# Transposing FFN activations on VectorE in squares of 32 instead of on TensorE, in a two-layer decoder trunk

## The chip, the core and the metric

The kernel runs on one core of a Trainium2 chip. The core has a matrix engine (TensorE, "PE" in the profile, with its weight loads as "PEld"), VectorE ("DVE"), ScalarE ("ACT"), GpSimd ("POOL"), and SyncE ("SP"), which here only issues DMA transfers. The metric is the device time of one execution in microseconds (us), lower is better; a run's number is the median of several executions.

## What is computed

The reference is a trunk of two layers on 256 tokens of width 2048, all in float32. What matters here is the dense SwiGLU feed-forward network (FFN) that ends each layer, with an inner width of 5632, and the projections around it:

```
for i in range(DEPTH):                       # DEPTH = 2
    mixer = even_mixer if i % 2 == 0 else odd_mixer
    h = h + mixer(rms_norm(h, ...), ...)
    h = h + swiglu(rms_norm(h, ffn_norm[i]), ffn_w_gate[i], ffn_w_up[i], ffn_w_down[i])
return rms_norm(h, final_norm)

def swiglu(hn, w_gate, w_up, w_down):
    return (jax.nn.silu(hn @ w_gate) * (hn @ w_up)) @ w_down
```

The even mixer is attention beside a gated delta rule, the odd mixer a gated MLP over positions; the change touches neither.

## The kernel before

The 256 tokens are two token tiles of 128 partitions (`NT` = 2). Widths are cut into chunks of 512 (`CW`): the model's 2048 are 4 chunks (`NCH`), the FFN's 5632 are 11 (`NFF`). A matmul contracts over partitions, so what is multiplied by a weight must lie with its features on the partitions: it must be transposed. The kernel calls such a transposed chunk a unit: for each token tile a pair of tiles of 128 features by 4 blocks by 128 tokens, a high part rounded to the reduced type `fp32r` and a low part with the rest (`split`: ScalarE casts `hi`, VectorE subtracts to get `lo`).

`dense` multiplies units by weights. For each unit it loads a piece `raw` of 512 rows of weights (1 MB, by SP, 3 buffers), and for each of its 4 blocks of 128 rows splits it: ScalarE casts `whi`, VectorE subtracts to get `wlo` (6 buffers each). TensorE then does three matmuls for each token tile (high by high, high by low, low by high), so six for each block, each 128 by 128 against 512 columns.

`ffn` runs over the 11 chunks: `dense` with the gate weights, SiLU on ScalarE into `sg`, `dense` with the up weights, a multiplication on VectorE (SCALAR_TENSOR_TENSOR) into `sg`, and `fill_unit`, which makes the unit of the chunk. `fill_unit` transposes with TensorE, four blocks of 128 by 128 for each token tile against the identity matrix `ident` into the PSUM buffers `side`, and then splits. `project` is the down projection (and the mixers' output projections): for each of 4 chunks of the output one `dense` over all units, an addition into the residual `h`, and, unless it is the last layer, `fill_unit` of the new residual with the next norm's gain, which makes the next stage's units.

No engine's order is written by hand. Every operation is recorded with a planned cost and a priority (`prio`; lower goes first among operations that are ready), and `plan` simulates engines, DMA and buffers, and fixes each engine's order and each tile's buffer. Weight splits have priority 0, `fill_unit` and what surrounds it 1, matmuls of `dense` 9. A tile gets a buffer only when one is free, and when all tiles recorded before it can still be held: an operation that is recorded late but waits for nothing, such as the load of the final norm's gain (`load_final`, `swdge` on POOL), may start as soon as that allows. There are 58 buffers `unit` and 4 `wide`, each of 4 KB on a partition at the most.

All operations are issued from one line (178, the recorder's call), so the profile's groups differ by tile names, not by lines.

Of the kernel before, what the change touches and what calls it, by code (L numbers as in the profile page):

```python
# [10 lines left out]
F32R = mybir.dt.float32r  # L11
BF16 = mybir.dt.bfloat16
AF = mybir.ActivationFunctionType
ALU = mybir.AluOpType
AX = mybir.AxisListType

P = 128
D = 2048
SEQ = 256
NT = SEQ // P  # L20
KB = 4
CW = 512
NCH = D // CW
# [29 lines left out]
NFF = DFF // CW  # L53
# [8 lines left out]
C_TRI, C_TB, C_SU, C_H0, C_DMASK, C_ONE, C_AM, C_LVL, C_UP, C_SAME, C_DIAG = 0, 1, 2, 3, 4, 5, 6, 8, 10, 11, 12  # L62
NCONST = 16
LAG = 10
SB = 16


# [208 lines left out]
class Engine:  # L276
# [5 lines left out]
    def __getattr__(self, name):  # L282
        f = getattr(self.engine, name)

        def record(*args, **kw):
            aps = [a for a in (*args, *kw.values()) if isinstance(a, bass.AP)]
            size = lambda a: a.free_size()
            n, k, table, nbytes = size(aps[0]), self.key, None, 0
            scalars = sum(size(a) == 1 for a in aps[1:])
            if name == "dma_start":  # L290
                cost, nbytes = (1040.0 if k == "pool" else 60.0), 4 * P * n
            elif k == "pe":
                cost = 3.0 + (107.0 if name == "transpose" else
                              (1.0 if aps[1].dtype == F32R and n >= 256 else 4.0) * n / 2.4)
            elif k == "act":
                given = sum(not isinstance(kw.get(x, 0.0), float) for x in ("scale", "bias"))
                cost = (51.0 if aps[1].space == bass.MemoryType.PSUM else 93.0) + 0.833 * n + 93.0 * given
                if name == "activation":
                    table = self.schedule.TABLES.get(args[2])
                    cost += 93.0 * ("accum_out" in kw)  # L300
            elif k == "dve":
                n = size(aps[1]) if name in ("tensor_reduce", "bn_stats") else n
                cost = 69.0 + (0.521 if name == "tensor_scalar" else 1.042) * n + 60.0 * scalars
            else:
                cost = 165.0 * n + 320.0 if ALU.pow in args else 1.9 * n + 200.0
            self.schedule.record(k, f, args, kw, cost, table, nbytes)

        return record
# [6 lines left out]
class Trunk:  # L315
# [135 lines left out]
    def fill_unit(self, srcs, gain=None):  # L451
# [10 lines left out]
            self.split(ps, unit[t])  # L462
        return unit


    def dense(self, w, units, off, width=CW, pcs=None, lag=0, first=False):

        nc = self.nc  # L470
        ps = [self.bank(width) for _ in range(NT)]
        pcs = range(len(units)) if pcs is None else pcs
        size = P * KB * width
        todo = deque()

        def product(t, x, k, hi, lo, st, sp):
            xh, xl = x[t]
            nc.tensor.matmul(ps[t], xh[:, k], hi, start=st, stop=False)
            nc.tensor.matmul(ps[t], xh[:, k], lo, start=False, stop=False)
            nc.tensor.matmul(ps[t], xl[:, k], hi, start=False, stop=sp)  # L480

        for unit, pc in zip(units, pcs):
            with self.prio(2 * pc - 19 if first else 0):
                raw = self.slot((P, KB, width), F32, "raw")
                o = off + pc * size
                nc.sync.dma_start(raw, w[o:o + size].rearrange("(p k n) -> p k n", p=P, k=KB))
            for k in range(KB):
                with self.prio(0):
                    tags = ("unit", "unit") if lag and k % 2 else ("whi", "wlo")
                    hi, lo = [self.slot((P, width), F32R, tag) for tag in tags]  # L490
                    nc.scalar.copy(hi, raw[:, k])
                    nc.vector.tensor_tensor(lo, raw[:, k], hi.bitcast(F32), ALU.subtract)
                with self.prio(9):
                    todo.append((unit, k, hi, lo, pc == pcs[0] and k == 0, pc == pcs[-1] and k == KB - 1))
                    product(0, *todo[-1])
                    if len(todo) > lag:
                        product(1, *todo.popleft())
        with self.prio(9):
            for x in todo:
                product(1, *x)  # L500
        return ps
# [6 lines left out]
    def project(self, w, units, gain, pcs=None):  # L508

        self.begin_norm()  # L510
        size = D * CW if pcs is not None else len(units) * KB * P * CW
        for n in range(NCH):
            self.residual(n, self.dense(w, units, n * size, pcs=pcs, lag=LAG if gain is None and n == NCH - 1 else 0))
            with self.prio(1):
                if gain is not None:
                    self.units.append(self.fill_unit([self.h[t][n] for t in range(NT)], gain[:, KB * n:KB * (n + 1)]))
                self.chunk_stats(n)
                if gain is None:
                    for t in range(NT):
                        self.nc.vector.tensor_tensor(self.h[t][n], self.h[t][n], self.gf[n], ALU.mult)  # L520
# [176 lines left out]
    def delta_inverse(self, u):  # L697


        nc = self.nc  # L700
        nb = P // SB

        wide = self.wide([P, 4, SB, SB])

        def masked(um, c):
            nc.vector.tensor_tensor(um, u, self.ct[c].unsqueeze(1).to_broadcast([P, 4, P]), ALU.mult)
            return um

        uc = self.slot((P, 4, SB), F32, "uc")
        um = masked(self.unit(), C_UP)  # L710
        nc.vector.tensor_reduce(uc, um.rearrange("p h (b i) -> p h i b", b=nb), AX.X, ALU.add)
        diag = self.ct[C_DIAG][:, :SB]
        parts = [self.slot((P, 4, SB), F32R, "ucp") for _ in range(2)]
        self.split(uc, parts)
        for h in range(0, 4, 2):
            ps = self.side(P, 2, SB * SB)
            for i, engine in enumerate((nc.vector, nc.gpsimd)):
# [268 lines left out]
    def ffn(self, i, gain):  # L986
        nc = self.nc
        units, act = self.units, []
        for n in range(NFF):
            pg = self.dense(self.t[f"gate{i}"], units, n * D * CW)  # L990
            with self.prio(1):
                if n == 0:
                    self.end_norm()
                sg = [self.unit(shape=(P, CW)) for _ in range(NT)]
                for t in range(NT):
                    nc.scalar.activation(sg[t], pg[t], AF.Silu, scale=self.rstd[t])
            pu = self.dense(self.t[f"up{i}"], units, n * D * CW)
            with self.prio(1):
                for t in range(NT):
                    nc.vector.scalar_tensor_tensor(sg[t], pu[t], self.rstd[t], sg[t], ALU.mult, ALU.mult)  # L1000
                act.append(self.fill_unit(sg))
        if gain is None:
            self.load_final()
        self.project(self.t[f"down{i}"], act, gain)
# [138 lines left out]
```

## Time and profile before

| | |
|---|---|
| time, median of 3 runs | 2188.32 us (2188.25 to 2190.48) |
| the profiled execution: its time, its span | 2188.75 us, 2186.7 us |
| PE, PEld busy | 2166.3 us (99%), 1792.4 us (82%) |
| DVE, ACT, POOL busy | 1326.0 us (61%), 1138.5 us (52%), 59.0 us (3%) |
| mean granted TensorE clock | 0.999 |
| the even mixer, about | 0 to 355 us |
| first FFN: gate and up, down | 355 to 932.6 us, 932.6 to 1175.7 us |
| the odd mixer | 1175.7 to 1451.6 us |
| second FFN: gate and up, down and the end | 1451.6 to 1940.4 us, 1940.4 to 2186.7 us |

The span runs from the first instruction to the last; the profiled execution's time is 2.05 us longer, and it is 0.43 us above the median of the runs. Matmuls overlap: a row's mean duration (say 390 ns) is from its start to its modelled end, while the next one starts after 227 ns, so TensorE's cost is read from starts, not from durations. In a row of the timeline "x4" are four instructions that follow each other.

### The profile page before, as it was taken

Reading aid. Unit: us, or ns where it says so; the run is one execution under the profiler, and the core shown is the slowest. Engines: PE = TensorE matmul, PEld = TensorE weight load, DVE = VectorE, ACT = ScalarE, POOL = GpSimd, SP = SyncE. Lnnn points to the kernel's source line nnn. Section 1 sums busy time; section 2 is a strip of 40 time slices with the busy share of each in tenths; the row PEclk is TensorE's granted clock in tenths of the full one; section 3 lists DMA queues with packets and bytes.
Section 4 is the critical chain, followed back from the end, with each engine's and each line's share of the span. In section 5 each row is a group of like instructions: output and inputs, shape, how many; then the busy total and the mean of one; then the engine's idle time right before and its main releaser. Section 6 shows DMA issues by size and latency. Waiting matters only on the chain.

```text
span 2186.7 us, 27199 instructions
## 1 busy us (share of the span) xinstructions
PE 2166.3 (99%) x10044; PEld 1792.4 (82%) x10044; DVE 1326.0 (61%) x2265; ACT 1138.5 (52%) x2034; POOL 59.0 (3%) x68
## 2 busy tenths in 40 slices
PE   8999999999999999999999999999999999999998
PEld 7787888888888888888888888888888888888886
DVE  8796886765555555555555576665555555555553
ACT  7665654554545554444445545554555445444453
POOL 1010100000000000000010000000000000000000
PEclk9999999999999999999999999999999999999999
DMA  7342435555555555555565555555555555565553
GB/s 250 123 156 76 154 117 172 182 186 191 192 193 193 184 187 189 192 193 193 192 237 186 196 168 186 178 189 192 193 185 187 189 192 191 192 209 194 194 195 132
DMA packets 58453, 399.07 MB, mean 183 GB/s; under 512 B 6976, under 2 KB 7232, under 8 KB 11216
## 3 DMA queue, kind: packets, MB, share of 16 engines
q1 hardware_dynamic: 57168, 393.61, 53.0%
q0 software_dynamic: 1152, 3.74, 0.5%
q8 instruction: 78, 1.28, 0.2%
q14 instruction: 55, 0.45, 0.1%
HBM read 395.22 MB, written 2.10 MB: 182 GB/s over the span
## 4 chain that ended last, share of the span: by engine, by line
PE 96%; DVE 2%; ACT 1%; issue 1%; DMA 0%; POOL 0%; SPq 0%; POOLq 0%; DVEq 0%; ACTq 0%
PE mm L178 90%; PE side L178 6%; DVE unit L178 1%; DVE wlo L178 1%; ACT whi L178 0%; DMA h<-in_x 0%; ACT junk L178 0%; POOL unit L178 0%; DVE uc L178 0%; SPq L178 0%; DVE yt L178 0%; DVE h L178 0%; DVE yr L178 0%; ACT L178 0%; ACT unit L178 0%
## 5 line engine op out<-in xcount | busy, mean ns | idle before, releaser
L178 PE MATMUL mm<-whi,unit 128*128 128x512 f32 (+1 forms) x5864 | 1829.8, 391 | 0.0
L178 DVE TENSOR_TENSOR wlo<-raw,whi 128x512 fp32r<-128x512 f32 (+1 forms) x1466 | 1011.0, 691 | 806.0 <-ACT whi L178 800.7
L178 ACT CAST whi<-raw 128x512 fp32r<-128x512 f32 (+1 forms) x1466 | 909.1, 621 | 938.6 <-DVE wlo L178 752.6
L178 PEld LDWEIGHTS mm<-whi,unit 128*128 128x128 f32 x5864 | 1097.8, 188 | 226.0 <-issue 4.7
L178 PE MATMUL mm<-wlo,unit 128*128 128x512 f32 (+1 forms) x2932 | 1140.9, 390 | 0.0
L178 PEld LDWEIGHTS mm<-wlo,unit 128*128 128x128 f32 x2932 | 551.1, 188 | 110.8 <-issue 0.2
L178 PE MATMUL side<-unit,unit 128*128 128x128 f32 (+3 forms) x448 | 60.6, 285 | 0.0
L178 PEld LDWEIGHTS side<-unit,unit 128*128 128x128 f32 (+2 forms) x448 | 54.4, 182 | 5.6 <-issue 1.4
L178 ACT ACTIVATE unit<-mm,rstd 128x512 f32<-128x512 f32 (+1 forms) x84 | 56.1, 671 | 2.2
L178 PE MATMUL side<-ident,unit 128*128 128x128 f32 x356 | 55.0, 273 | 0.4 <-DVE unit L178 0.4
L178 PEld LDWEIGHTS side<-ident,unit 128*128 128x128 f32 x356 | 44.1, 140 | 12.2 <-issue 2.3
L178 DVE TENSOR_TENSOR unit<-side,unit 128x512 fp32r<-128x512 f32 (+1 forms) x64 | 43.6, 690 | 10.8 <-ACT unit L178 10.2
L178 ACT CAST unit<-side 128x512 fp32r<-128x512 f32 x60 | 35.1, 586 | 19.5 <-PE side L178 17.5
L178 DVE TENSOR_TENSOR unit<-unit,unit 128x512 fp32r<-128x512 f32 (+1 forms) x56 | 39.7, 714 | 1.0
L178 PE MATMUL mm<-unit,unit 128*128 128x512 f32 x132 | 35.9, 389 | 0.0
L178 ACT COPY unit<-side 128x512 f32<-128x512 f32 (+1 forms) x36 | 20.6, 585 | 25.4 <-PE side L178 25.4
L178 DVE SCALAR_TENSOR_TENSOR unit<-side,conv,unit 128x255 f32<-128x255 f32 (+2 forms) x72 | 31.1, 473 | 2.4 <-ACT unit L178 2.4
L178 ACT ACTIVATE junk<-h 128x512 bf16<-128x512 f32 x40 | 25.1, 628 | 11.1 <-DVE h L178 8.4
L178 DVE SCALAR_TENSOR_TENSOR unit<-mm,rstd,unit 128x512 f32<-128x512 f32 x44 | 30.9, 743 | 0.0
L178 DVE TENSOR_TENSOR h<-mm,h 128x512 f32<-128x512 f32 x40 | 25.8, 683 | 6.3 <-PE mm L178 6.3
L178 PEld LDWEIGHTS mm<-unit,unit 128*128 128x128 f32 x132 | 24.8, 188 | 5.1
L178 PE MATMUL side<-ident,h 128*128 128x128 f32 x128 | 20.7, 291 | 7.3 <-DMA h<-in_x 7.3
(119 smaller groups left out, 461.4 us busy)
## 6 DMA issues: line engine op xcount, KB each, us to landing
raw<-in_gate SPq DMA_DIRECT2D x88, 1024.0 KB, 4.8
raw<-in_up SPq DMA_DIRECT2D x88, 1024.0 KB, 4.8
raw<-in_down SPq DMA_DIRECT2D x88, 1024.0 KB, 4.9
raw<-in_even_in SPq DMA_DIRECT2D x40, 1024.0 KB, 4.9
raw<-in_odd_in SPq DMA_DIRECT2D x32, 1024.0 KB, 4.9
raw<-in_even_out SPq DMA_DIRECT2D x16, 1024.0 KB, 4.8
raw<-in_odd_out SPq DMA_DIRECT2D x16, 1024.0 KB, 4.9
raw<-in_even_in SPq DMA_DIRECT2D x4, 544.0 KB, 6.7
```

The costliest lines, as they stand in the source:

```text
L178: f(*map(real, args), **{k: real(a) for k, a in kw.items()})
```

## The change

A new function `turn` transposes on VectorE. Its instruction transposes squares of 32 by 32: for each of the 16 pairs of a group of 32 source partitions and a group of 32 target partitions it issues one instruction that takes all such squares of the chunk, for both token tiles at once where the source holds both. `sg` becomes one `wide` tile for both token tiles, so that an FFN chunk takes 16 instructions of 32 partitions by 256 elements (2 token tiles by 4 blocks by 32). The result is in SBUF, and `turned_unit` splits it from there. This replaces `fill_unit` in `ffn` for all chunks but the last of each layer, and in the first layer's down projection for the first three of the four residual chunks: there `turn` is called for each token tile, 16 instructions of 32 by 128 elements each, and the gain is multiplied in place. The planner is given a price for the new instruction.

```
--- before.py
+++ after.py
@@ -62,6 +62,7 @@
 LAG = 10
+SQ = 32
 SB = 16
@@ -300,7 +301,7 @@
             elif k == "dve":
                 n = size(aps[1]) if name in ("tensor_reduce", "bn_stats") else n
-                cost = 69.0 + (0.521 if name == "tensor_scalar" else 1.042) * n + 60.0 * scalars
+                cost = (183.0 if name == "transpose" else 69.0) + (0.521 if name == "tensor_scalar" else 1.042) * n + 60.0 * scalars
@@ -460,6 +461,27 @@
+    def turn(self, src):
+
+        n = src.shape[1]
+        out = self.wide([P, n, KB, P]) if n > 1 else self.unit(shape=(P, n, KB, P))
+        blocks = src.rearrange("p n (k c) -> p n k c", k=KB)
+        for i in range(0, P, SQ):
+            for j in range(0, P, SQ):
+                self.nc.vector.transpose(out[j:j + SQ, :, :, i:i + SQ].rearrange("p n k c -> p (n k) c"),
+                                         blocks[i:i + SQ, :, :, j:j + SQ].rearrange("p n k c -> p (n k) c"))
+        return out
+
+    def turned_unit(self, turned, gain=None):
+
+        unit = []
+        for t, x in enumerate(turned):
+            if gain is not None:
+                self.nc.vector.tensor_tensor(x, x, gain.unsqueeze(2).to_broadcast([P, KB, P]), ALU.mult)
+            unit.append([self.unit(F32R), self.unit(F32R)])
+            self.split(x, unit[t])
+        return unit
@@ -513,7 +535,11 @@
                 if gain is not None:
-                    self.units.append(self.fill_unit([self.h[t][n] for t in range(NT)], gain[:, KB * n:KB * (n + 1)]))
+                    hs, gs = [self.h[t][n] for t in range(NT)], gain[:, KB * n:KB * (n + 1)]
+                    if len(units) > NCH and n < NCH - 1:
+                        self.units.append(self.turned_unit([self.turn(x.unsqueeze(1))[:, 0] for x in hs], gs))
+                    else:
+                        self.units.append(self.fill_unit(hs, gs))
@@ -991,14 +1017,18 @@
-                sg = [self.unit(shape=(P, CW)) for _ in range(NT)]
+                sg = self.wide([P, NT, CW])
                 for t in range(NT):
-                    nc.scalar.activation(sg[t], pg[t], AF.Silu, scale=self.rstd[t])
+                    nc.scalar.activation(sg[:, t], pg[t], AF.Silu, scale=self.rstd[t])
             pu = self.dense(self.t[f"up{i}"], units, n * D * CW)
             with self.prio(1):
                 for t in range(NT):
-                    nc.vector.scalar_tensor_tensor(sg[t], pu[t], self.rstd[t], sg[t], ALU.mult, ALU.mult)
-                act.append(self.fill_unit(sg))
+                    nc.vector.scalar_tensor_tensor(sg[:, t], pu[t], self.rstd[t], sg[:, t], ALU.mult, ALU.mult)
+                if n < NFF - 1:
+                    turned = self.turn(sg)
+                    act.append(self.turned_unit([turned[:, t] for t in range(NT)]))
+                else:
+                    act.append(self.fill_unit([sg[:, t] for t in range(NT)]))
```

Three places show what the planner makes of it. The first is TensorE just after the first layer's first FFN chunk, where `side` are the transposes of both token tiles, set between the first matmuls of the next chunk. Before:

```order
L178 MATMUL mm_3688_9392<-wlo_3695_9356,unit_3136_8714 128x512
L178 MATMUL side_3673_9410<-ident_0_0_4484,unit_3537_9216 128x128 x4
L178 MATMUL mm_3688_9392<-whi_3694_9351,unit_3137_8721 128x512
L178 MATMUL side_3679_9420<-ident_0_0_4484,unit_3538_9226 128x128 x4
L178 MATMUL mm_3691_9399<-whi_3694_9351,unit_3143_8725 128x512
```

Now:

```order
L179 MATMUL mm_3696_9345<-wlo_3703_9309,unit_3136_8668 128x512
L179 MATMUL mm_3696_9345<-whi_3702_9304,unit_3137_8675 128x512
L179 MATMUL mm_3699_9352<-whi_3702_9304,unit_3143_8679 128x512
L179 MATMUL mm_3699_9352<-wlo_3703_9309,unit_3143_8679 128x512
L179 MATMUL mm_3699_9352<-whi_3702_9304,unit_3144_8689 128x512
```

The eight transposes are gone there, as at 23 such places in all, and the matmuls keep their order. From the first FFN on, the two kernels' TensorE orders differ in nothing else.

The second place is VectorE after a middle chunk of the first FFN (its seventh). `wide_5265` is `sg`, `wide_5401` the transposed chunk, the rows on `wlo` are the weight splits. Before:

```order
L178 SCALAR_TENSOR_TENSOR unit_5217_11400<-mm_5222_11404,rstd_0_3533_9065,unit_5217_11400 128x512
L178 SCALAR_TENSOR_TENSOR unit_5218_11410<-mm_5225_11412,rstd_0_3536_9096,unit_5218_11410 128x512
L178 TENSOR_TENSOR wlo_5408_11589<-raw_5398_11483,whi_5407_11579 128x512
L178 TENSOR_TENSOR wlo_5416_11598<-raw_5398_11483,whi_5415_11591 128x512
L178 TENSOR_TENSOR unit_5358_11610<-side_5353_11594,unit_5357_11602 128x512
L178 TENSOR_TENSOR unit_5364_11619<-side_5359_11604,unit_5363_11612 128x512
```

Now, the first rows:

```order
L179 SCALAR_TENSOR_TENSOR wide_5265_11390<-mm_5270_11394,rstd_0_3533_9019,wide_5265_11390 128x512
L179 SCALAR_TENSOR_TENSOR wide_5265_11390<-mm_5273_11401,rstd_0_3536_9050,wide_5265_11390 128x512
L179 TENSOR_TENSOR wlo_5464_11578<-raw_5454_11472,whi_5463_11568 128x512
L179 STREAM_TRANSPOSE wide_5401_11585<-wide_5265_11390 32x8x32
L179 TENSOR_TENSOR wlo_5472_11589<-raw_5454_11472,whi_5471_11580 128x512
L179 STREAM_TRANSPOSE wide_5401_11585<-wide_5265_11390 32x8x32
L179 TENSOR_TENSOR wlo_5480_11599<-raw_5454_11472,whi_5479_11592 128x512
L179 STREAM_TRANSPOSE wide_5401_11585<-wide_5265_11390 32x8x32 x2
L179 TENSOR_TENSOR wlo_5489_11614<-raw_5487_11514,whi_5488_11603 128x512
```

The 16 transposes stand one or two at a time between 11 weight splits, and the chunk's own split follows after the eleventh; before it followed after the second. In the first down projection 32 transposes stand in the same way, two or three at a time, between 14 weight splits.

The third place is at the start of the program, which the diff does not touch: SP's loads. `raw` are the weights of the first `dense` (four pieces of 544 KB), `h` the tokens, `ctab`, `conv`, `rows` and `bs` the mixer's tables. Before:

```order
L178 DMA h_0_52_4508<-in_x 128x512
L178 DMA h_0_53_4510<-in_x 128x512
L178 DMA raw_175_4575<-in_even_in 128x1088
L178 DMA unit_222_4579<-in_ctab 128x512
L178 DMA unit_223_4582<-in_ctab 128x512
```

Now:

```order
L179 DMA h_0_53_4464<-in_x 128x512
L179 DMA unit_222_4525<-in_ctab 128x512
L179 DMA unit_223_4527<-in_ctab 128x512
L179 DMA unit_224_4529<-in_ctab 128x512
L179 DMA unit_225_4531<-in_ctab 128x512
L179 DMA conv_0_228_4533<-in_conv 128x96
L179 DMA rows_0_229_4536<-in_rows 128x160
L179 DMA bs_0_230_4540<-in_bs 128x8
L179 DMA raw_175_4543<-in_even_in 128x1088
```

The fourth piece of weights now comes behind the tables. What moved it is POOL: with `sg` out of the `unit` buffers the planner finds one of these free for the whole program up to the second FFN, and issues the first of the four loads of the final gain (256 KB) as POOL's first work; before all four stood after the odd mixer. A second one moved to the first FFN. On TensorE this exchanges some neighbours in the first 320 rows of about 9,200, the even mixer's first part; from there to the first FFN the order is the same.

## The prediction

> **What bounds the kernel now.** I read the page's head first, then the chain of waits, then one FFN chunk by timeline and by windows.
>
> ```profile
> span 2186.7 us, 27199 instructions
> PE 2166.3 (99%) x10044; PEld 1792.4 (82%) x10044; DVE 1326.0 (61%) x2265; ACT 1138.5 (52%) x2034; POOL 59.0 (3%) x68
> PE 96%; DVE 2%; ACT 1%; issue 1%; DMA 0%; POOL 0%; SPq 0%; POOLq 0%; DVEq 0%; ACTq 0%
> ```
>
> The first two rows are the head, the third the chain that ended last, by engine. TensorE is never long without work. Busy records of matmuls overlap, though, so the chain in order of time has to show what an FFN chunk is made of (start, duration, what):
>
> ```profile
> 709.31 0.44 PE side L178 x4
> 709.98 0.44 PE side L178 x4
> 710.42 43.33 PE mm L178 x191
> 753.75 0.44 PE side L178 x4
> 754.42 0.44 PE side L178 x4
> 754.86 43.34 PE mm L178 x191
> 992.27 0.44 PE side L178 x4
> ```
>
> From 710.42 to 754.86 is one period, 44.44 us: 192 matmuls and 8 transposes, nothing else. The 192 at the pace of 43.33/191 = 0.2269 us make 43.56; the transposes take 2 x 0.44 = 0.88, so 0.11 us each. The same places in TensorE's timeline (start, duration, records):
>
> ```profile
> 708.92 0.40 PE L178 MATMUL mm<-wlo,unit 128*128 128x512 f32 x1
> 709.15 0.60 PE L178 MATMUL side<-ident,unit 128*128 128x128 f32 x4
> 709.51 0.48 PE L178 MATMUL mm<-whi,unit 128*128 128x512 f32 x1
> 709.82 0.60 PE L178 MATMUL side<-ident,unit 128*128 128x128 f32 x4
> 710.18 0.48 PE L178 MATMUL mm<-whi,unit 128*128 128x512 f32 x1
> 710.49 0.39 PE L178 MATMUL mm<-wlo,unit 128*128 128x512 f32 x1
> 710.72 0.62 PE L178 MATMUL mm<-whi,unit 128*128 128x512 f32 x2
> ```
>
> By starts, 709.15 to 710.72 is 1.57 us, of which three matmuls are 0.68: again 0.89 for eight transposes. A transpose's own duration, 0.27 us, would say 2.2; it overlaps its neighbours. TensorE waits for nothing here, so whatever leaves its queue leaves the span.
>
> **What is removed.** 10 chunks in each of 2 layers and 3 residual chunks: 23 places with eight transposes, 23 x 0.88 = **20.2 us**. The down projection pays the same: its row at 992.27, the last quoted of the chain, ends its first output chunk.
>
> **What is added on VectorE**, and whether it stays covered. How VectorE and ScalarE stand against TensorE between two chunks:
>
> ```profile
> 710.40:754.90 44.50, 44.50 (x202) 36.90 (x201) 24.79 (x37) 22.40 (x37) 0.00 (x0) 1.00 0.56 189
> L178 DVE TENSOR_TENSOR wlo<-raw,whi 128x512 fp32r<-128x512 f32 x32 | 22.1, 692 | 19.5 <-ACT whi L178 19.4
> L178 ACT CAST whi<-raw 128x512 fp32r<-128x512 f32 x32 | 20.0, 624 | 21.6 <-DVE wlo L178 20.6 <-PE mm L178 0.9
> 750.61 0.62 ACT L178 CAST whi<-raw 128x512 fp32r<-128x512 f32 x1 [0.74 <-DVE wlo L178]
> 751.26 0.69 DVE L178 TENSOR_TENSOR wlo<-raw,whi 128x512 fp32r<-128x512 f32 x1 [0.67 <-ACT whi L178]
> 751.88 1.40 DVE L178 SCALAR_TENSOR_TENSOR unit<-mm,rstd,unit 128x512 f32<-128x512 f32 x2
> 753.20 1.48 DVE L178 TENSOR_TENSOR wlo<-raw,whi 128x512 fp32r<-128x512 f32 x2
> ```
>
> The first row is a window of one chunk (PE, PEld, DVE, ACT, POOL busy; the clock 1.00; DMA 56%). VectorE works 24.8 us of 44.4, so there is room for 16 instructions of up to about (43.5 - 24.8)/16 = 1.17 us. But they come in a burst. A weight block comes every 6 x 0.227 = 1.36 us, its `wlo` takes 0.69, so 0.67 is free in each. `whi` has 6 buffers: a cast starts when TensorE has left the block six before, so its block is used five blocks, 6.8 us, later. The pair of cast and subtraction is done 1.4 us after its start (0.62 and 0.69 and the gaps), which leaves a **lead of 5.4 us** by which VectorE may be late before TensorE stops.
>
> The trace has no transpose on VectorE. The nearest rows, by the 256 and 128 elements that each partition streams:
>
> ```profile
> L178 DVE TENSOR_TENSOR unit<-ucp,unit 128x256 fp32r<-128x256 f32 x16 | 8.3, 529 | 0.0
> L178 DVE SCALAR_TENSOR_TENSOR unit<-side,bs,unit 128x256 f32<-128x256 f32 x16 | 7.1, 477 | 0.2
> L178 DVE TENSOR_SCALAR unit<-unit,gp 128x128 fp32r<-128x128 f32 x16 | 5.8, 404 | 0.0
> L178 DVE SCALAR_TENSOR_TENSOR unit<-side,br,unit 128x128 f32<-128x128 f32 x48 | 14.2, 342 | 0.0
> L178 DVE TENSOR_TENSOR unit<-yr,unit 128x128 f32<-128x128 f32 x16 | 3.7, 282 | 0.0
> L178 DVE TENSOR_REDUCE uc<-unit 128x64 f32<-128x512 f32 x4 | 4.2, 1053 | 0.0
> L178 DVE TENSOR_REDUCE a<-unit 128x4 f32<-128x512 f32 x4 | 2.7, 682 | 0.0
> ```
>
> Between 282 (128) and 692 (512 elements) an element costs 1.07 ns over a fixed 0.145 us, so 256 cost at least 0.42. The last two rows read the same 512 elements, one in long strides and one straight: strides cost a factor 1.54, and 0.477 x 1.54 = 0.74 is my upper bound for a transposing read in short rows; 1.05 is the dearest row there is. I take 0.53, the ordinary two-operand row. For 128 elements: 0.28 to 0.62, taken 0.34.
>
> The order has 16 transposes among 11 `wlo` after the two multiplications. Time there: 11 x 1.36 = 15.0. Work: 1.40 + 11 x 0.69 + 16 x 0.53 = 17.5. VectorE ends 2.5 us late, inside 5.4; then 0.67 free in each block makes it up in four blocks. Threshold: 16 T = 15.0 + 5.4 - 1.4 - 7.6, T = 0.71 us. At the lower bound it is 0.7 late, at 0.74 TensorE would stop for about 0.5 in a chunk. Queued behind the late transposes are the later `wlo`, and on ScalarE the chunk's two `unit` casts hold the next `whi` casts; both have the same 5.4 us. The finished unit itself is wanted only in the down projection, tens of us later in all but the last chunk, which stays on TensorE. In the down projection 32 transposes stand among 14 `wlo`: 19.0 us of time against two residual additions 1.4 + 9.7 + 32 x 0.34 = 22.0, late by 3.0; the threshold is 0.42, and at 0.62 it would stop 6.4 us, three times. Cost taken: **0**, from -0 to 10 in the chunks and 0 to 19 in the down projection. If the cover were gone, each 0.1 us on a transpose would cost 1.6 us a chunk, 32 in all.
>
> [...]
>
> The splits now read SBUF instead of PSUM, on rows that differ by little:
>
> ```profile
> L178 ACT CAST unit<-side 128x512 fp32r<-128x512 f32 x60 | 35.1, 586 | 19.5 <-PE side L178 17.5
> L178 ACT CAST unit<-unit 128x512 fp32r<-128x512 f32 x32 | 19.6, 617 | 9.6 <-DVE unit L178 9.6
> ```
>
> 0.03 us on an engine that is half idle: 0, hidden by ScalarE's 0.74 in each block.
>
> **What is moved: the start.** The first final-gain load (256 KB) joins the loads at the start, and the fourth piece of weights goes behind about 1.13 MB of tables on SP's queue.
>
> ```profile
> 10.61 0.33 SPq L178 DMA_DIRECT2D raw<-in_even_in  x1
> 10.98 1.94 SPq L178 DMA_DIRECT2D unit<-in_ctab  x4
> 4.58 1.94 PE L178 MATMUL side<-ident,h 128*128 128x128 f32 x8 [4.58 <-DMA h<-in_x]
> 6.00:8.00 2.00, 0.53 (x3) 0.12 (x1) 1.75 (x4) 1.24 (x2) 0.00 (x0) 1.00 0.96 309
> 12.00:14.00 2.00, 2.00 (x14) 2.00 (x14) 1.10 (x3) 0.80 (x4) 0.00 (x0) 1.00 1.05 413
> 19.37 0.41 ACT L178 CAST whi<-raw 128x272 fp32r<-128x272 f32 x1
> 23.18 0.52 PE L178 MATMUL mm<-whi,unit 128*128 128x272 f32 x2
> ```
>
> TensorE starts on DMA, and DMA is full (0.96, then 1.05 of 16 engines). 256 KB at 309 GB/s are 0.8 us, paid in full if they come before the tokens, not at all if after. 1.13 MB at 413 GB/s put the fourth piece 2.7 us later; its first cast ran at 19.37 and its first matmul at 23.18, 3.8 us later (less about 1 us of cast and subtraction), so this is nearly hidden: 0 to 3. Later waits of the even mixer may shift either way by a us. Taken: **+1**, from -1 to +4.
>
> **Sum.** 2186.7 - 20.2 + 0 + 1 = 2167.5 us of span. The profiled execution took 2.05 more than its span: 2169.5, and it was 0.4 above the median of the runs: **2169**, 0.9% less.
>
> **The rivals.** (1) *VectorE's burst stops TensorE.* Place: the later `wlo` after each chunk. From T = 0.71 it takes part of the gain back, from 0.77 (16 T = 15.0 + 5.4 + 0.9 - 9.0) the chunk is slower than before. At the dearest row's 1.05 a chunk stops for 5.4 and gains 0.88: 20 x 4.5 = +90; at half of it for half the elements a residual chunk stops for 32 x 0.53 - 13.4 = 3.5 and gains 0.88: +8 for three. With the start's +1 about 2287. For it: no row shows this instruction, and its writes are rows of 32. Against: all straight rows of 256 lie below 0.53. (2) *ScalarE and VectorE pace TensorE, not the other way round.* `whi` waits for `wlo` and `wlo` for `whi`, and 0.62 + 0.69 + two gaps make 1.36, TensorE's own period. If that loop were real, 16 x 0.53 = 8.5 us of transposes would go into it at each chunk: 20 x (8.5 - 0.9) = +152, 2340. Against: a wait for `wlo` six blocks back ends long before, so the row names the wrong engine, and starved matmuls would start unevenly once in six, while they start every 0.227. (3) *The start eats more*: the fourth piece is not hidden and a chain of the even mixer breaks, +5 more: 2174. (4) *The transposes cost TensorE nothing*, hidden under the matmuls' weight loads, and nothing is gained: 2189. Against: the period sums to 192 matmuls and 0.88.
>
> **Chances.** Forecast 0.74. (1) 0.10, in half of it a part of the gain is left (some 2180) and in half it is slower; (2) 0.03; (3) 0.09; (4) 0.04. Less than 0.2% (4.4 us) cannot be told from no change in a measurement of this kernel. Faster: 0.74 + 0.09 + 0.04 of (1) = 0.87; the same: (4) and 0.01 of (1), 0.05; slower: 0.05 + 0.03 = 0.08. The range goes from 2166 (start at -1, all covered, 1 below) to 2179 (a us of stops in the down projections, half a us in each chunk, or the start at +5); the cases above it hold about 0.15.
>
> **What would show it.** Right: the FFN period falls from 44.44 to 43.55, TensorE has no `side` row between chunks and still no wait, VectorE's busy time grows by about 20 x 16 x 0.53 + 3 x 32 x 0.34 = 203 us to some 1530, the transposes measure 0.42 to 0.71, the even mixer ends within 4 us of where it did. Wrong: waits of `mm` for `wlo` after a chunk (1), a period above 51 (2), idle TensorE near 23 us (3), a period still at 44.4 (4).

## The result and the profile after

The changed kernel takes 2168.49 us (median of 5 runs, 2168.44 to 2168.93) against 2188.85 for the kernel before in the same session (5 runs, 2188.25 to 2190.48). The ratio is 0.9908, with a 95% interval from 0.9897 to 0.9920: **0.9% faster**, 20.4 us. The forecast was 2169.

The head of the page after, and its chain of waits by engine:

```profile
span 2166.9 us, 27246 instructions
PE 2145.5 (99%) x9860; PEld 1774.7 (82%) x9860; DVE 1483.9 (68%) x2681; ACT 1133.6 (52%) x2034; POOL 55.7 (3%) x68
PE 96%; DVE 2%; DMA 1%; issue 1%; ACT 1%; SPq 0%; POOL 0%; POOLq 0%; DVEq 0%; ACTq 0%
```

TensorE has 184 matmuls fewer, 23 x 8, and stays 99% busy; the chain still runs through it. VectorE has 416 instructions more, 20 x 16 and 3 x 32, and went from 61% to 68%. The chain in order of time (start, duration, what), at the points where a stage begins. Before:

```profile
355.33 51.94 PE mm L178 x229
...
443.78 43.33 PE mm L178 x191
...
932.62 59.66 PE mm L178 x263
...
1175.66 93.88 PE mm L178 x414
...
1451.58 43.33 PE mm L178 x191
```

Now:

```profile
356.78 51.94 PE mm L179 x229
...
445.22 478.54 PE mm L179 x2111
...
924.87 239.17 PE mm L179 x1055
...
1165.14 93.88 PE mm L179 x414
...
1440.99 478.53 PE mm L179 x2111
```

The first row of each is not yet the FFN, though the table of the kernel before counts it in: from 355.33 (now 356.78) the even mixer's output projection runs, 88.45 us before and 88.44 now, and the FFN's own matmuls begin at 443.78 (now 445.22). In the FFN, where before a pair of `side` pieces stood every 44.44 us, one piece of 2111 matmuls now covers ten chunk boundaries. Its pace is 478.54/2111 = 0.2267 us, so a chunk of 192 matmuls takes 43.52. The gain by stage follows from starts in the two chains. Output projection and first FFN up to the FFN's last transposes: before 932.62 - 355.33 = 577.29, now 924.87 - 356.78 = 568.09, **9.20 less, ten times 0.92**. First down projection: before 1175.66 - 932.62 = 243.04, now 1165.14 - 924.87 = 240.27, 2.77 less, three times 0.92. The second FFN's ten places gave 9.20 again (from 1451.58 to 1940.42, now from 1440.99 to 1920.63), 21.2 in all. The output projection begins at 356.78 instead of 355.33, so the start took 1.45 back: 21.2 - 1.45 = 19.75, and the spans differ by 19.8. The odd mixer took 275.9 us in both, and the stretch behind the second FFN's last transposes 246.3.

What TensorE waited for in the changed kernel (total us, times, longest), all rows of its waits:

```profile
PE side L179 <- DMA h<-in_x: 8.1, 2, 7.4
PE side L179 <- DVE unit L179: 3.3, 4, 1.5
PE side L179 <- ACT junk L179: 0.9, 2, 0.4
```

Before, the same three rows had 7.3, 3.0 and 0.9. There is no row of `mm` for `wlo`: VectorE's new work never stopped TensorE. What that work costs, by groups with their shapes (busy us, mean ns of one, idle before):

```profile
L179 DVE STREAM_TRANSPOSE wide<-wide 32x256 f32<-32x256 f32 x320 | 139.4, 436 | 7.6
L179 DVE STREAM_TRANSPOSE unit<-h 32x128 f32<-32x128 f32 x96 | 29.0, 302 | 1.9
```

And VectorE's timeline just after a middle chunk (start, duration, what, idle before):

```profile
747.19 0.69 DVE L179 TENSOR_TENSOR wlo<-raw,whi 128x512 fp32r<-128x512 f32 x1 [0.67 <-ACT whi L179]
...
762.13 0.89 DVE L179 STREAM_TRANSPOSE wide<-wide 32x256 f32<-32x256 f32 x2
763.05 0.69 DVE L179 TENSOR_TENSOR wlo<-raw,whi 128x512 fp32r<-128x512 f32 x1
...
768.99 0.69 DVE L179 TENSOR_TENSOR wlo<-raw,whi 128x512 fp32r<-128x512 f32 x1 [0.66 <-ACT whi L179]
```

The beat of the weight blocks is 1.36 us. The eleventh `wlo` after the one at 747.19 was due at 747.19 + 11 x 1.36 = 762.15 and started at 763.05, 0.9 late. By 768.99 VectorE waits its usual 0.66 for ScalarE again. In the same stretch ScalarE's timeline reads:

```profile
761.49 0.62 ACT L179 CAST whi<-raw 128x512 fp32r<-128x512 f32 x1 [0.74 <-PE mm L179]
762.85 0.62 ACT L179 CAST whi<-raw 128x512 fp32r<-128x512 f32 x1 [0.74 <-PE mm L179]
764.25 0.63 ACT L179 CAST unit<-wide 128x512 fp32r<-128x512 f32 x1 [0.77 <-DVE wide L179]
```

The casts keep to 1.36 us exactly while `wlo` is late, so VectorE is not what they wait for. Before, the same 0.74 was put down to VectorE's `wlo`; now that `wlo` comes late, the row names TensorE, which releases the buffer. As the beat is the same, TensorE must have been the cause before, too.

### The profile page after: what moved, and what is told of

The parts are those of the page before. It is cut to its first block, busy times and chain, and to the rows that moved or that the text cites. A ratio compares the mean times of both kernels' runs of the same rounds, so it can differ in the third digit from the quotient of the medians.

```text
span 2166.9 us, 27246 instructions
## 1 busy us (share of the span) xinstructions
PE 2145.5 (99%) x9860; PEld 1774.7 (82%) x9860; DVE 1483.9 (68%) x2681; ACT 1133.6 (52%) x2034; POOL 55.7 (3%) x68
## 4 chain that ended last, share of the span: by engine, by line
PE 96%; DVE 2%; DMA 1%; issue 1%; ACT 1%; SPq 0%; POOL 0%; POOLq 0%; DVEq 0%; ACTq 0%
PE mm L179 90%; PE side L179 5%; DVE unit L179 1%; DVE wlo L179 1%; DMA raw<-in_even_in 1%; DMA h<-in_x 0%; ACT junk L179 0%; ACT whi L179 0%; DVE uc L179 0%; SPq L179 0%; DVE yt L179 0%; DVE yr L179 0%; DVE h L179 0%; POOL unit L179 0%; ACT L179 0%
## 5 line engine op out<-in xcount | busy, mean ns | idle before, releaser
L179 DVE STREAM_TRANSPOSE wide<-wide 32x256 f32<-32x256 f32 x320 | 139.4, 436 | 7.6
L179 ACT CAST unit<-wide 128x512 fp32r<-128x512 f32 x40 | 24.8, 620 | 15.3 <-DVE wide L179 15.3
L179 DVE SCALAR_TENSOR_TENSOR wide<-mm,rstd,wide 128x512 f32<-128x512 f32 x44 | 30.9, 743 | 0.0
L179 ACT ACTIVATE wide<-mm,rstd 128x512 f32<-128x512 f32 x44 | 30.2, 686 | 0.4
L179 DVE STREAM_TRANSPOSE unit<-h 32x128 f32<-32x128 f32 x96 | 29.0, 302 | 1.9
L179 PE MATMUL side<-ident,unit 128*128 128x128 f32 x180 | 28.6, 273 | 0.4 <-DVE unit L179 0.4
```

Source lines behind the costliest of these rows:

```text
L179: f(*map(real, args), **{k: real(a) for k, a in kw.items()})
```

## The experiments

The theory: each place costs TensorE the start-to-start time of its eight transposes, VectorE has a lead of some 5 us that its burst must not use up, and the start costs what the early load of the final gain does to the first tokens. The rivals are those of the prediction: the burst stops TensorE; VectorE and ScalarE set the pace; the start breaks for another reason. All experiments change a few lines of the changed kernel, and all times of the kernel before were taken beside them.

### Which part gives what: chunks only, residual units only

FFN chunks alone:

```diff
-                    if len(units) > NCH and n < NCH - 1:
+                    if False:
```

> VectorE transposes only the FFN chunks; the first down projection's three residual units go back to TensorE. Theory (each group of eight transposes costs TensorE 0.92 us wherever it stands, as the FFN period now says): 3 x 0.92 = 2.8 us lost, 2171.3. Rival (the residual units' transposes are covered by the down projection, or VectorE's 32 instructions for each cost as much as they save): 2168.5.

Measured: 2171.14 us (2171.06 to 2171.24), 2.65 above the changed kernel, where three places at 0.92 make 2.77.

Residual units alone (the FFN's `sg` and `fill_unit` as before):

```diff
-                sg = self.wide([P, NT, CW])
+                sg = [self.unit(shape=(P, CW)) for _ in range(NT)]
...
-                if n < NFF - 1:
-                    turned = self.turn(sg)
-                    act.append(self.turned_unit([turned[:, t] for t in range(NT)]))
-                else:
-                    act.append(self.fill_unit([sg[:, t] for t in range(NT)]))
+                act.append(self.fill_unit(sg))
```

> Only the three residual units are transposed on VectorE, the FFN chunks stay on TensorE; the activations stay in their old buffers, so the start is planned as before the change. Theory: 3 x 0.92 = 2.8 us below the kernel before: 2185.6 to 2186.1. Rival (nothing to gain there): 2188.3 to 2188.9.

Measured: 2185.59 us (11 runs, 2185.03 to 2186.93), ratio 0.9987 (0.9978 to 0.9996): 2.7 below the kernel before, again three times 0.92. So the places add up one by one, whatever engine work goes with them. Here `sg` is in the `unit` buffers, no gain load stands at the start, and the even mixer's output projection begins at 355.05, close to the 355.33 before.

### The start: the final gain's load after the odd mixer

```diff
+            self.schedule.early = 1500000.0
             self.load_final()
+            self.schedule.early = 0.0
```

> The changed kernel, but the four loads of the final gain may not be planned before the odd mixer is over, as they were before the change; TensorE's order is then that of the kernel before with the 23 groups of transposes taken out. Theory (the re-ordered start costs TensorE 1.45 us, the shift of the first FFN's beginning between the two traces, and nothing makes it up): 2167.0 us, 1.4 below the changed kernel's 2168.5, and the first FFN begins at 355.3 again. Rival (the shift is chance of the execution, or belongs to the new FFN): 2168.5.

Measured: 2166.31 us (2166.09 to 2166.81), 2.2 below the changed kernel and 0.7 below what was expected. TensorE's order is then that of the kernel before without the 23 places, and so is the order of SP's loads at the start. POOL's is not: freed of the gain, the planner puts another of POOL's loads first, 64 KB for the mixer (`ltri`), which the kernel before issued at 913 us. TensorE's first work in the changed kernel, by timeline:

```profile
7.45 1.94 PE L179 MATMUL side<-ident,h 128*128 128x128 f32 x8 [7.45 <-DMA h<-in_x]
10.06 1.97 PE L179 MATMUL side<-ident,h 128*128 128x128 f32 x8 [0.67 <-DMA h<-in_x]
```

With the load late:

```profile
4.89 1.94 PE L179 MATMUL side<-ident,h 128*128 128x128 f32 x8 [4.89 <-DMA h<-in_x]
7.66 1.97 PE L179 MATMUL side<-ident,h 128*128 128x128 f32 x8 [0.83 <-DMA h<-in_x]
```

And the second of these rows before:

```profile
9.27 1.97 PE L178 MATMUL side<-ident,h 128*128 128x128 f32 x8 [2.74 <-DMA h<-in_x]
```

The first tokens are in 2.6 us sooner. What counts is the second group of tokens, without which TensorE cannot go on: in the four traces without the gain at the start (before, this one, residual units alone, and the run with all edits further down) its transposes start between 7.66 and 9.27 (mean 8.66), in the six with it between 10.06 and 10.29 (mean 10.13), 1.5 later. One start differs from another by chance, too: the even mixer's output projection began at 355.33, 354.23, 355.05 and 355.55 in the four (mean 355.0), and between 356.46 and 357.37 in the six (mean 356.85). The load's price is the difference, **1.8 us**; by the medians of the runs it is 2.2, or 1.7 if each kernel is set against the kernel before of its own session. I had priced it at 256 KB by the rate of the moment, 0.8. Windows of 1 us from 3 to 6 us show what was missing for the first tokens (last two columns: share of the DMA engines, GB/s). The changed kernel:

```profile
3.00:4.00 1.00, 0.00 (x0) 0.00 (x0) 0.00 (x0) 0.00 (x0) 0.00 (x0) 1.00 0.77 114
4.00:5.00 1.00, 0.00 (x0) 0.00 (x0) 0.00 (x0) 0.00 (x0) 0.00 (x0) 1.00 0.94 162
5.00:6.00 1.00, 0.00 (x0) 0.00 (x0) 0.00 (x0) 0.00 (x0) 0.00 (x0) 1.00 0.91 286
```

With the load late:

```profile
3.00:4.00 1.00, 0.00 (x0) 0.00 (x0) 0.00 (x0) 0.00 (x0) 0.00 (x0) 1.00 0.60 221
4.00:5.00 1.00, 0.11 (x1) 0.14 (x2) 0.00 (x0) 0.22 (x1) 0.00 (x0) 1.00 1.10 418
5.00:6.00 1.00, 1.00 (x6) 1.00 (x7) 0.00 (x0) 0.97 (x3) 0.00 (x0) 1.00 1.03 415
```

The DMA engines are almost as busy, but move 562 KB in these 3 us instead of 1054 (937 in the kernel before, where POOL loads nothing at the start). The missing 492 KB are 1.2 us at 415 GB/s; if the gain's own 256 KB fall into the same stretch, 0.6, that makes an estimate of 1.8 of the first tokens' 2.6. The DMA view of the first 12 us has a part of the reason: the packets of the gain, 0.26 MB on POOL's queue, took 14.9% of the 16 engines' time, those of SP's queue 63.2% for 2.88 MB. Per byte that is 2.6 times as much. Why they take so long stays open. The other thing that moved at the start, the fourth piece of weights behind the tables, was undone by the same edit, so its share was not measured alone. Its first cast ran at 22.53 instead of 19.37, but the trace speaks for a hidden delay: from the second eight token transposes to the first 512-wide `mm` TensorE took 27.49 - 10.06 = 17.4 us in the changed kernel, 17.2 before and 17.8 with the load late.

### The burst: a planner that thinks transposes cheap

```diff
-                cost = (183.0 if name == "transpose" else 69.0) + (0.521 if name == "tensor_scalar" else 1.042) * n + 60.0 * scalars
+                cost = 5.0 if name == "transpose" else 69.0 + (0.521 if name == "tensor_scalar" else 1.042) * n + 60.0 * scalars
```

The same instructions, but the planner puts the transposes in long runs. TensorE's order by tiles is that of the changed kernel in this run and in the next one, so what differs is the order on the other engines.

> The same work as the changed kernel; only the planner's price of a transpose is set to 5 ns, so that it puts the 16 of a chunk into two bursts with one weight split between them, and the 32 of a residual unit almost together. Theory (VectorE may be 5.4 us late, no more): to the end of the next weight split but one VectorE needs 1.40 + 3 x 0.69 + 16 x 0.45 = 10.7 us for 3 x 1.36 = 4.1, and the chunk's two subtractions follow: late by 6.6 to 7.3, so TensorE stops 1.2 to 1.9 us in each of 20 chunks and about 3 us at each of three residual units: 2168.5 + 33 to 47 = 2201 to 2216. Rival (VectorE is 68% busy, and the order of its work does not matter): 2168.5.

Measured: 2219.72 us (2219.34 to 2220.8), ratio 1.0143 (1.0129 to 1.0157): **slower than the kernel before**. The wait that was foretold is there, in TensorE's waits:

```profile
PE mm L179 <- DVE wlo L179: 33.0, 43, 4.2
```

VectorE after a chunk:

```profile
711.63 0.69 DVE L179 TENSOR_TENSOR wlo<-raw,whi 128x512 fp32r<-128x512 f32 x1 [0.67 <-ACT whi L179]
...
714.16 1.78 DVE L179 STREAM_TRANSPOSE wide<-wide 32x256 f32<-32x256 f32 x4
715.97 0.69 DVE L179 TENSOR_TENSOR wlo<-raw,whi 128x512 fp32r<-128x512 f32 x1
716.69 5.39 DVE L179 STREAM_TRANSPOSE wide<-wide 32x256 f32<-32x256 f32 x12
722.11 0.69 DVE L179 TENSOR_TENSOR wlo<-raw,whi 128x512 fp32r<-128x512 f32 x1
```

TensorE at the same time, and after the first down projection's first output chunk, where two runs of 16 transposes stand:

```profile
721.43 0.61 PE L179 MATMUL mm<-whi,unit 128*128 128x512 f32 x2
722.86 0.50 PE L179 MATMUL mm<-wlo,unit 128*128 128x512 f32 x1 [0.81 <-DVE wlo L179]
...
724.72 0.50 PE L179 MATMUL mm<-wlo,unit 128*128 128x512 f32 x1 [0.21 <-DVE wlo L179]
...
1007.86 0.61 PE L179 MATMUL mm<-whi,unit 128*128 128x512 f32 x2
1012.70 0.80 PE L179 MATMUL mm<-wlo,unit 128*128 128x512 f32 x1 [4.23 <-DVE wlo L179]
...
1017.83 0.40 PE L179 MATMUL mm<-wlo,unit 128*128 128x512 f32 x1
```

The first stop **measures the lead**. By its beat TensorE wanted that `wlo` at 721.43 + 2 x 0.227 = 721.88. The one three blocks before, written on the beat, was wanted three blocks sooner, 721.88 - 4.08 = 717.80, and was finished at 711.63 + 0.69 = 712.32. That leaves 5.5 us; the prediction worked out 5.4 from the six buffers. The chain's rows give the cost of a chunk:

```profile
724.72 12.33 PE mm L179 x53
769.85 12.33 PE mm L179 x53
...
1012.70 6.46 PE mm L179 x17
1079.39 5.60 PE mm L179 x17
1145.21 54.79 PE mm L179 x229
```

A chunk takes 45.13 us instead of 43.52, 1.61 more, 32 in twenty. An output chunk of the down projection takes 66.69 instead of 264 x 0.2267 = 59.85, 6.8 more, and the next 65.82, 6.0 more. From the first FFN's start to the odd mixer's the chain takes 755.98 (445.12 to 1201.10) instead of 719.92; less 16.1 for ten chunks that leaves 20.0 for the three stops of the down projection. Together 52.2, where the spans differ by 52.1. Of the 6.8 the wait is only 4.2; the rest comes afterwards. From 1012.70 to 1017.83 twelve matmuls start in 5.13 us, not in 2.72. Windows at the short and at the long stop say why (the third number from the end of a row is the granted TensorE clock):

```profile
722.00:724.00 2.00, 1.19 (x6) 0.97 (x6) 1.97 (x5) 1.89 (x4) 0.00 (x0) 1.00 0.21 25
...
1012.00:1014.00 2.00, 1.30 (x3) 1.11 (x4) 2.00 (x5) 1.86 (x4) 0.00 (x0) 0.50 0.51 70
1014.00:1016.00 2.00, 2.00 (x6) 1.52 (x6) 2.00 (x4) 2.00 (x5) 0.00 (x0) 0.50 0.72 307
1016.00:1018.00 2.00, 2.00 (x7) 1.57 (x6) 2.00 (x4) 0.70 (x2) 0.00 (x0) 0.59 0.65 188
1018.00:1020.00 2.00, 2.00 (x10) 1.61 (x10) 0.92 (x3) 1.04 (x2) 0.00 (x0) 1.00 0.80 279
```

After the stop of 4.23 us the granted clock is 0.50 for about 5 us; the stop of 0.81 leaves it at 1.00. At what length of a stop the clock falls was not shown. The slow clock costs 2.4 us here (5.13 - 2.72). Behind the other two stops the chain's rows, 17 matmuls in 5.60 us and 229 in 54.79, hold 1.7 and 2.9 more than the pace of 0.2267 makes; by the same count the row of the first stop, 6.46, holds 2.6, and the three hold 7.2. This was not in the expectation; the measurement lies 4 above its upper end.

### Is VectorE still free? Every transpose twice

```diff
-        for i in range(0, P, SQ):
+        for i in (*range(0, P, SQ), *range(0, P, SQ)):
```

> Every VectorE transpose is issued twice into the same place (416 more instructions of 0.44 and 0.30 us, 168 us of work); the planner spreads them over more weight splits. Theory (VectorE is covered as long as it is not late by more than 5.4 us in one place): the same time, 2168.5 within 0.5, with VectorE busy some 1652 us, 76%. Rival (VectorE's load as such holds TensorE up): over 2175.

Measured: 2168.58 us (2168.17 to 2169.11), against 2168.49 with single ones. The page's head and the group of the FFN's transposes:

```profile
PE 2145.7 (99%) x9860; PEld 1774.5 (82%) x9860; DVE 1648.2 (76%) x3097; ACT 1132.4 (52%) x2034; POOL 58.8 (3%) x68
```

```profile
L179 DVE STREAM_TRANSPOSE wide<-wide 32x256 f32<-32x256 f32 x640 | 278.7, 435 | 14.8
```

VectorE is busy for 164 us more (1648.2 against 1483.9), at no cost in time. If VectorE and ScalarE set the pace, as rival (2) had it, this would have cost about as much. Together with the cheap price it shows what counts: not how much is put on VectorE, but how much at a stretch. At the usual price, 183 + 1.042 x 256 = 450 ns against the 436 measured, the planner sets the 32 transposes of a chunk one or two at a time between the `wlo`, from 750.14 to 779.14 in the trace.

### More of the same: the last chunk, the odd mixer, everything together

The FFN's last chunk too:

```diff
-                if n < NFF - 1:
+                if n < NFF:
```

> The last FFN chunk of each layer is also transposed on VectorE (22 chunks instead of 20). Theory (its unit is wanted only by the eleventh piece of the down projection, some 54 us later): 2 x 0.92 = 1.8 us less, 2166.7. Rival (the first down projection's unit comes late, or buffers run short there): 2168.5 or more.

Measured: 2166.99 us (2166.59 to 2167.45), 1.5 less for two places more (2 x 0.92 = 1.84). In the traces the two stages concerned are 0.92 and 0.99 shorter.

The odd mixer's four gated chunks too:

```diff
-                us = [self.unit(shape=(P, CW)) for _ in range(NT)]
+                both = self.wide([P, NT, CW])
+                us = [both[:, t] for t in range(NT)]
...
-                act.append(self.fill_unit(us))
+                turned = self.turn(both)
+                act.append(self.turned_unit([turned[:, t] for t in range(NT)]))
```

> The odd mixer's four gated chunks are also transposed on VectorE, 16 instructions each. Gain on TensorE 4 x 0.92 = 3.7 us. But a chunk there is one dense of 96 matmuls, 21.8 us, in which VectorE has 16 x 0.69 + 4 x 0.48 + 16 x 0.45 + 2 x 0.69 = 21.5 us to do, and 15.4 us of the layer norm fall into the same four chunks. Theory (the cover is VectorE's free time at the place): it is gone here, VectorE falls behind, and waits of TensorE eat the gain: 2166 to 2180. Rival (spare time of the kernel as a whole counts, VectorE is 68% busy): 2164.8.

Measured: 2165.93 us (2164.97 to 2166.03), 2.6 less, of 4 x 0.92 = 3.7. The expectation, 2166 to 2180, was wrong in its mechanism: the cover is nearly used up here, but not gone. The window of 88 us over the four chunks, with PE, PEld and DVE as the first three busy times:

```profile
1276.00:1364.00 88.00, 87.76 (x387) 72.20 (x386) 80.56 (x151) 46.84 (x78) 0.00 (x0) 1.00 0.54 186
```

VectorE is busy for 80.6 of the 88, and TensorE still lacks only 0.24, in one stop for a `wlo` at 1362.10. I had put all of the layer norm's VectorE work into the chunks with the transposes; nearly all of it runs before this window (15 of its 16 multiplications and additions with the norm's tables). In the traces the mixer got 3.2 shorter (from 1165.74 to 1438.39, against 1165.14 to 1440.99). The 0.5 that is missing from 3.7 is about what the one stop costs, if it costs 0.3 more than its 0.24 as the short stops of the cheap price did. The medians show 2.6, within their scatter of a us.

All three edits, the late gain load, the last chunk and the odd mixer:

> The final gain's loads kept behind the odd mixer, and the two last FFN chunks and the odd mixer's four gated chunks transposed on VectorE as well. Theory (the parts lie in different places and TensorE's queue sets the time in each, so they add up): 2168.5 - 2.2 (loads) - 1.5 (last chunks) - 2.6 (odd mixer), each as its own run measured, 2162.2 +- 1. Rival (VectorE, busier everywhere, takes part back): 2164 or more.

Measured: **2162.00 us** (2161.07 to 2162.45), ratio 0.9876 (0.9859 to 0.9892) to the kernel before, 6.5 below the changed kernel; the three gains alone add up to 2.2 + 1.5 + 2.6 = 6.3. It beats both kernels. By the page's head TensorE has 48 matmuls fewer than in the changed kernel, 9812, six places of eight, and is still 99% busy; VectorE is busy for 70%.

## Why the prediction was right, and where its sizes were off

**What bounds the kernel** was read rightly. The gain is the number of places taken out of TensorE's queue times their start-to-start time, shown by the stage sums and by both one-part kernels.

**What is removed** was mis-sized: 0.88 a place, measured 0.92, so 21.2 and not 20.2. I counted the two `side` pieces of 0.44 and took the matmuls' pace from pieces that border on them, 43.33/191 = 0.2269. The undisturbed pace is 0.2267; on 192 matmuls that is the missing 0.04. So a place of transposes also slows the matmuls beside it a little, and a period compared with an undisturbed one contains that.

**What is added on VectorE**: taken at nothing, measured at nothing. The transposes took 0.436 and 0.302 us against 0.53 and 0.34 taken, near the lower bounds of 0.42 and 0.28; nothing measured lay near the uppers, 0.74 and 0.62. So the strided reduction was the wrong neighbour: 128 elements more cost 0.134 us, 1.05 ns each, about what straight rows pay (1.07). The lateness of 0.9 follows from the prediction's own sum with the measured time: 1.40 + 11 x 0.69 + 16 x 0.436 - 15.0 = 1.0. VectorE's busy time is 1484 and not 1530 mostly for the same reason (139.4 + 29.0 = 168 instead of 203). The other 10 us are not work saved: the durations of all its other instructions add up to 1393 in both kernels, but records that follow each other without a break overlap a little (the `wlo` at 747.19 ends at 747.88, 0.08 after the next instruction starts), and the busy time counts that once. The 5.4 us of lead was worked out and not seen; the cheap price showed it (5.5).

**The splits from SBUF**: nothing, as taken. The `unit` cast at 764.25 takes 0.63 and waits for VectorE, as the last row of ScalarE's timeline shows, and TensorE feels nothing of it.

**The start** was placed rightly and mis-sized: +1 taken, +1.45 in this trace, +1.8 over the ten traces, +2.2 by the medians with and without the load. The 0.8 for 256 KB took for granted that the load costs its bytes; in the first 12 us its packets held the DMA engines 2.6 times as long per byte as the others. The fourth piece of weights was hidden as far as the trace tells.

**The sum** came out 0.5 us from the measured time, and that is in part luck. In this trace the gain was 1.0 larger than taken and the start 0.45 dearer. The profiled execution took 1.72 more than its span and not 2.05, and stood 0.13 above the median and not 0.4. As a difference the forecast was 1 us off: 2188.3 - 2169 = 19.3 against 20.4 measured beside the kernel before. The terms were right to 5% in the large one and to a factor of about two in the small one.

**The rivals.** (1) The burst is a real mechanism, with the price and the threshold given, and it makes the kernel slower; at 0.436 us and with the transposes spread it did not arise. What decides is as much the planner's price of a transpose as its length: with 5 ns in its table instead of the right order of size the same instructions lose 51 us. (2) is refuted twice, by casts that keep their beat while `wlo` is late and by the doubled transposes. (3) is refuted beyond 2 us. (4) is refuted by the period of 43.52.

## What to carry to other kernels

Where one engine's queue sets the time, price an instruction in it by the period with and without it, not by its duration and not by its own pieces; here a transpose of 0.27 us was worth 0.115. Before work is moved to an engine with idle time, work out how late that engine may be, from the buffers between it and the bound, and how the work is spread: 168 us more of transposes in small pieces were free, and the original amount in runs of 12 and 16 cost 51 us. And look at what the freed buffers let the scheduler move to the start, where a transfer ahead of the first input can cost more than its bytes: 1.8 us here, where the bytes made 0.8.

## What the runs showed that was not expected

A small load at the program's start cost more than its bytes: with 256 KB of final gain issued by POOL ahead, the DMA engines were 0.77 to 0.94 busy and moved 114 to 286 GB/s in the three us from 3 to 6, against 221 to 418 without it; the first tokens came 2.6 us later, and about 1.8 of that stayed. A single stop of TensorE of 4.2 us cost 6.8, since the granted clock then stood at 0.50 for about 5 us. Stops of 0.8 us had no such price, but a short stop costs about 0.3 more than its wait row shows (1.61 for two stops of 0.81 and 0.21): the row counts from the modelled end of the matmul before, 0.17 after the next one was due, and the step behind a stop is 0.11 longer.
